# Loading a mask in 2.5 KB runs, behind the weights and both halves of the first load, with zero matmuls between the first blocks

## Chip, cores, metric

The kernel runs on one core of a Trainium2 chip. The metric is the device time of one execution in microseconds, lower being better. Executions that are called fast (not in a slow state) are compared with fast executions of the kernel before, on the same chip and in the same rounds. The profile's span is 1.6 us shorter than the time: 89.0 against 90.6 us for the kernel before.

## The reference, cut to what matters

```python
x:      (16, 512, 512) float32      weight: (512, 512) float32
scale:  0.125                       mask:   (512, 512) float32, 1 strictly below the diagonal, else 0
y = scale * matmul(x, weight)
y = where(mask == 1, y, -1e9)
return softmax(y, axis=-1)
```

The kernel relies on the mask's block shape. Of the 512 x 512 mask it reads only the four 128 x 128 blocks on the diagonal. What lies above them is a constant, and what lies below is unmasked.

## The kernel before

x is read in eight groups of 2 MB; a group is worked on in two halves of four row slots, called units here, sixteen in all. For each unit, VectorE casts to bf16, TensorE transposes (16 matmuls against the identity), VectorE and ScalarE copy the result out of PSUM (where this kernel's matmuls put it), and TensorE multiplies by W and adds the mask's "band" as one more matmul. ScalarE takes the exponential with its sum, VectorE normalises, and a DMA stores. All DMAs are issued by the SP engine, in program order.

The loads at the start:

```python
load(0, slots(0))                       # first half of group 0, 1 MB
DP = P // S                             # 16 partitions
for b in range(KT):                     # 4 mask blocks
    r = b * P
    seq(nc.sync.dma_start(diag_f32[b * DP : (b + 1) * DP],
        mask[r : r + P, r : r + P].rearrange("(p t) c -> p t c", t=S)))   # 128 pieces of 512 B
seq(nc.sync.dma_start(w_f32, weight.rearrange("(p kt) n -> p kt n", kt=KT)))   # 1 MB
load(0, slots(1))                       # second half of group 0, 1 MB
for g in range(1, X_BUFS):              # X_BUFS = 5: four more groups of 2 MB
    load(g)
```

The first units. `spin(n)` issues n matmuls of zeros, meant to raise TensorE's clock.

```python
spin(12)
...                                     # identity, band constants, spread matrices
cast(0); transpose(0); evict(0)
# diag_bf = bias made of the mask: (1 - mask) * -512, in bf16
for h in range(2):
    for j in range(2):
        pm = spread[:, h] x diag_bf[:, slots(j)]          # a matmul places the rows
        # two copies, VectorE then ScalarE, from pm into the band
w_bf = bf16(w_f32)                      # half on VectorE, half on ScalarE
cast(1)
for u in range(U + 1):                  # U = 16 units
    transpose(u + 1); cast(u + 2); evict(u + 1); multiply(u); normalise(u - 1); ...
```

TensorE runs in this order, so the multiplication of unit u + 1 stands behind the transposes of unit u + 2.

The softmax here doesn't subtract the row's maximum and nothing guards it: scores larger than these inputs give would overflow.

## Time and profile before

| | kernel before |
|---|---|
| time, median of 3 runs | 90.63 us (90.41 to 90.82) |
| span of the profile | 89.0 us |
| bytes moved by DMA | 34.95 MB, 392 GB/s over the span |
| TensorE busy | 72.1 us, 81% of the span |

In the strip of 40 slices a digit is the busy share in tenths, PEclk the clock that TensorE was granted, GB/s what the DMA engines moved. In the table by stretches, each row gives the busy time of PE, PEld, DVE, ACT and POOL with the number of instructions, and at its end the granted clock, the DMA share and the GB/s. Where a high DMA share stands beside low GB/s, the packets took longer: in the changed kernel the share is 1.06 at 133 GB/s from 11 to 12 us, with mask packets of 290 to 365 ns (medians) where the first had taken 102 ns. The prediction shows the lines.

### The profile page before, as it was taken

The page shows a single profiled execution, that of the slowest core. Times are in us where ns is not written, and L with a number is a line of the kernel's source. Part 1 is how long each engine was busy: PE and PEld are TensorE (multiplying, and loading weights), DVE is VectorE, ACT ScalarE, POOL GpSimd, SP SyncE. Part 2 cuts the span into 40 slices and gives each one's busy share as a digit, 9 for nine tenths or more (in the row PEclk, how much of TensorE's full clock was granted, in tenths as well). Part 3 has the DMA queues.
Part 4 walks back from the last instruction along what each step waited for, and adds up shares of the span by engine and source line. Part 5 has one row for each costly group of instructions (what it writes and reads, how often), then busy time and mean ns, then how long its engine had stood idle before and what let it go on. Part 6 is the DMA issues. An engine that isn't in the chain of part 4 may idle for free.

```text
span 89.0 us, 1583 instructions
## 1 busy us (share of the span) xinstructions
PE 72.1 (81%) x585; PEld 49.6 (56%) x592; DVE 61.0 (68%) x121; ACT 55.9 (63%) x154; POOL 6.6 (7%) x14
## 2 busy tenths in 40 slices
PE   4994503999999999999999999999999999980000
PEld 1324103878955659995565999556599965530000
DVE  4856785079994877999687699977689880528000
ACT  5300593445977868698687779768777977671000
POOL 7940000000200000020000002000000200000000
PEclk9999855558999999999999999999999999999555
DMA  0998999999999999999998999999999999999770
GB/s 11 390 228 328 420 464 434 405 449 420 427 434 405 434 394 427 467 427 375 456 442 383 471 427 383 464 434 397 449 427 405 449 420 420 456 401 420 324 320 15
DMA packets 3462, 34.95 MB, mean 392 GB/s; under 512 B 384, under 2 KB 896, under 8 KB 896
## 3 DMA queue, kind: packets, MB, share of 16 engines
q1 hardware_dynamic: 3456, 34.87, 94.0%
q8 instruction: 4, 0.07, 0.3%
q14 instruction: 2, 0.02, 0.0%
HBM read 18.09 MB, written 16.78 MB: 392 GB/s over the span
## 4 chain that ended last, share of the span: by engine, by line
PE 73%; DMA 10%; SPq 4%; DVE 3%; issue 1%; ACT 1%; DVEq 0%; ACTq 0%
PE py L122 48%; PE pt L98 16%; DMA xf<-in_x_dram 10%; PE py L131 8%; SPq L174 3%; DVE ot L158 1%; DVE xb L89 1%; SPq L85 1%; ACT ot L141 1%; SPq L179 1%; DVEq L290 0%; DVE rinv L156 0%; ACTq L290 0%
## 5 line engine op out<-in xcount | busy, mean ns | idle before, releaser
L122 PE MATMUL py<-w_bf,xt 128*128 128x256 bf16 (+1 forms) x249 | 51.0, 334 | 0.4
L141 ACT ACTIVATE ot<-py 128x256 f32<-128x256 f32 (+1 forms) x64 | 31.2, 493 | 8.9 <-PE py L131 8.8
L122 PEld LDWEIGHTS <-xt 128*128 128x128 bf16 x256 | 25.3, 101 | 12.8
L109 ACT COPY xt<-pt 128x1024 bf16<-128x1024 bf16 x16 | 16.2, 1012 | 12.8 <-PE pt L98 8.0
L89 DVE CAST xb<-xf 128x2048 bf16<-128x2048 f32 x16 | 19.5, 1221 | 5.8 <-DMA xf<-in_x_dram 5.8
L158 DVE TENSOR_SCALAR ot<-ot,rinv 128x256 f32<-128x256 f32 (+1 forms) x64 | 23.0, 423 | 0.7
L98 PE MATMUL pt<-ident_bf,xb 128*128 128x128 bf16 x256 | 17.8, 225 | 5.1 <-DVE xb L89 5.1
L98 PEld LDWEIGHTS <-xb 128*128 128x128 bf16 x256 | 16.6, 116 | 7.5 <-DVE xb L89 6.7
L131 PE MATMUL py<-band,ident_bf 128*128 128x256 bf16 x64 | 17.9, 280 | 0.0
L108 DVE COPY xt<-pt 128x1024 bf16<-128x1024 bf16 x16 | 11.0, 688 | 7.8 <-PE pt L98 7.8
L141 ACT ACTIVATION_READ_ACCUMULATOR ot<-py 128x1 f32 x64 | 12.8, 201 | 0.0
L131 PEld LDWEIGHTS <-ident_bf 128*128 128x128 bf16 x64 | 6.5, 101 | 4.3
L160 POOL MEMSET ot<- 4x256 f32 x4 | 1.8, 448 | 63.1 <-DVE ot L158 63.1
L190 PE MATMUL py<-zeros 128*128 128x512 bf16 x12 | 5.3, 632 | 1.2 <-DVE zeros L185 1.2
L156 DVE RECIPROCAL rinv<-rsum 128x4 f32<-128x4 f32 x16 | 2.7, 168 | 5.1 <-ACT ot L141 5.1
L198 DVE MEMSET ot<- 128x2048 f32 x2 | 3.5, 1765 | 0.8 <-issue 0.8
L190 PEld LDWEIGHTS <-zeros 128*128 128x128 bf16 x12 | 1.6, 144 | 3.9 <-issue 2.8
L233 ACT CAST band<-py 64x512 bf16<-64x512 f32 x4 | 2.3, 580 | 1.1 <-DVE band L233 1.0
L233 DVE CAST band<-py 64x512 bf16<-64x512 f32 x4 | 2.5, 675 | 0.5 <-PE py L222 0.5
L222 PE MATMUL py<-diag_bf,spread 64*128 64x512 bf16 x4 | 1.2, 412 | 0.9 <-DVE diag_bf L209 0.9
L196 POOL MEMSET band<- 64x2048 bf16 x1 | 1.8, 1800 | 0.1
L195 POOL MEMSET band<- 64x2048 bf16 x1 | 1.8, 1802 | 0.0
(14 smaller groups left out, 6.6 us busy)
## 6 DMA issues: line engine op xcount, KB each, us to landing
xf<-in_x_dram SPq DMA_DIRECT2D x7, 2048.0 KB, 17.0
out_dram<-ot SPq DMA_DIRECT2D x6, 2048.0 KB, 13.8
out_dram<-ot SPq DMA_DIRECT2D x4, 1024.0 KB, 9.6
xf<-in_x_dram SPq DMA_DIRECT2D x2, 1024.0 KB, 7.2
w_f<-in_weight_dram SPq DMA_DIRECT2D x1, 1024.0 KB, 6.9
diag_f<-in_mask_dram SPq DMA_DIRECT2D x4, 64.0 KB, 4.9
```

The source lines that it names most:

```text
L89: seq(nc.vector.tensor_copy(xb, st_x[u // 2][:, slots(u)]))
L98: nc.tensor.transpose(st_pt[u][kt // 2][:, kt % 2, t], xb[:, t].rearrange("p (k kt) -> p kt k", kt=KT)[:, kt], ident_bf,)
L108: seq(nc.vector.tensor_copy(xt[:, 0:2], pt[0]))
L109: seq(nc.scalar.copy(xt[:, 2:4], pt[1]))
L122: nc.tensor.matmul(py[:, :NC], lhsT=xt[:, kt, t], rhs=w_bf[:, kt, :NC], start=(kt == 0), stop=(kt == KT - 1),)
L131: nc.tensor.matmul(py[:, h * HB : NC], lhsT=ident_bf, rhs=band[:, h, slots(u)][:, t], start=False, stop=True, skip_group_check=True,)
L141: nc.scalar.activation(out=ot[:, t, :NC], in_=py[:, :NC], func=AF.Exp, bias=0.0, scale=float(scale), accum_out=rsum[:, t : t + 1],)
L156: seq(nc.vector.reciprocal(rinv, st_sum.pop(u)))
L158: seq(nc.vector.tensor_scalar_mul(ot[:, t, :NC], ot[:, t, :NC], rinv[:, t : t + 1]))
L190: seq(nc.tensor.matmul(idle, lhsT=zeros[:, :P], rhs=zeros, start=True, stop=True))
L198: nc.vector.memset(ots[i][:, :, HB:], 0.0)
L233: copy(band[half, h, slots(j), g * P : (g + 1) * P], pm.rearrange("p (t c) -> p t c", t=T)[half],)
```

## The change

The intent: the mask's 512 B pieces are taken to be slow packets, so two pieces that are needed and what lies between them are read as one run of 2,560 B. Row r needs 128 columns and row r + 1 the same 128 columns, 2 KB further on. This gives half as many packets but 2.5 times the bytes (655 KB instead of 262 KB). The mask no longer stands ahead of W and the second half load; both come first. The work of the second unit is brought forward, and 14 + 8 zero matmuls fill TensorE's waits.

```diff
     load(0, slots(0))
+    seq(nc.sync.dma_start(w_f32, weight.rearrange("(p kt) n -> p kt n", kt=KT)))
+    load(0, slots(1))
     DP = P // S
+    RUN = N + P
+    diag_f32 = ots[OUT_BUFS - 1].rearrange("p t n -> p (t n)")[:HP, : S // 2 * RUN]
     for b in range(KT):
-        r = b * P
         seq(nc.sync.dma_start(
                 diag_f32[b * DP : (b + 1) * DP],
-                mask[r : r + P, r : r + P].rearrange("(p t) c -> p t c", t=S),
+                bass.AP(tensor=mask.tensor, offset=mask.offset + b * P * (N + 1),
+                        ap=[[2 * N, P // 2], [1, RUN]]),
         ))
-    seq(nc.sync.dma_start(w_f32, weight.rearrange("(p kt) n -> p kt n", kt=KT)))
-    load(0, slots(1))
...
     cast(0)
     transpose(0)
+    spin(14)
     evict(0)
-    (diag_bf: one tensor_scalar of 64 x 1024)
+    (w_bf: the two casts)
+    cast(1)
+    transpose(1)
+    spin(8)
+    evict(1)
+    (diag_bf: two tensor_scalars of 64 x 512, one for each piece of a run)
     (spread matmuls and band copies, unchanged)
-    (w_bf: the two casts)
-    cast(1)
     for u in range(U + 1):              # transpose and evict of unit 1 are left out here now
```

More of the change, by code (lines that the diff above doesn't have):

```diff
@@ L67 @@
     w_bf = const.tile([P, KT, N], BF16, name="w_bf")
-    diag_f32 = const.tile([HP, S, P], FP32, name="diag_f32")
     diag_bf = const.tile([HP, S, P], BF16, name="diag_bf")
@@ L175 @@
                 diag_f32[b * DP : (b + 1) * DP],
-                mask[r : r + P, r : r + P].rearrange("(p t) c -> p t c", t=S),
-            )
-        )
-    seq(nc.sync.dma_start(w_f32, weight.rearrange("(p kt) n -> p kt n", kt=KT)))
-    load(0, slots(1))
+                bass.AP(
+                    tensor=mask.tensor,
+                    offset=mask.offset + b * P * (N + 1),
+                    ap=[[2 * N, P // 2], [1, RUN]],
+                ),
+            )
+        )
     for g in range(1, X_BUFS):
@@ L206 @@
     transpose(0)
+    spin(14)
     evict(0)
-    seq(
-        nc.vector.tensor_scalar(
-            out=diag_bf,
-            in0=diag_f32,
-            scalar1=-MASK_NEG,
-            scalar2=MASK_NEG,
-            op0=ALU.mult,
-            op1=ALU.add,
+    seq(nc.vector.tensor_copy(w_bf[:, 0:2], w_f32[:, 0:2]))
+    seq(nc.scalar.copy(w_bf[:, 2:4], w_f32[:, 2:4]))
+    cast(1)
+    transpose(1)
+    spin(8)
+    evict(1)
+    for side in range(2):
+        seq(
+            nc.vector.tensor_scalar(
+                out=diag_bf.rearrange("k (j s) c -> k j s c", s=2)[:, :, side],
+                in0=diag_f32.rearrange("k (j c) -> k j c", c=RUN)[:, :, side * N : side * N + P],
+                scalar1=-MASK_NEG,
+                scalar2=MASK_NEG,
+                op0=ALU.mult,
+                op1=ALU.add,
+            )
         )
-    )
     for h in range(2):
@@ L237 @@
                 )
-    seq(nc.vector.tensor_copy(w_bf[:, 0:2], w_f32[:, 0:2]))
-    seq(nc.scalar.copy(w_bf[:, 2:4], w_f32[:, 2:4]))
-    cast(1)
     for u in range(U + 1):
-        if u + 1 < U:
+        if 2 <= u + 1 < U:
             transpose(u + 1)
@@ L246 @@
             cast(u + 2)
-        if u + 1 < U:
+        if 2 <= u + 1 < U:
             evict(u + 1)
```

## The prediction

> **What bounds the kernel now.** I read the strip of 40 slices first, then the chain that ended last, then the table by stretches, then the DMA packets. The strip:
>
> ```profile
> PE   4994503999999999999999999999999999980000
> PEclk9999855558999999999999999999999999999555
> DMA  0998999999999999999998999999999999999770
> GB/s 11 390 228 328 420 464 434 405 449 420 427 434 405 434 394 427 467 427 375 456 442 383 471 427 383 464 434 397 449 427 405 449 420 420 456 401 420 324 320 15
> ```
>
> One slice is 2.2 us. Two rows are full from slice 9 on: PE, and DMA at about 425 GB/s. So the kernel has two bounds that lie on each other, and only a change that shortens both can shorten it much. The visible slack is in the first slices (GB/s 228, PE idle and at half clock) and in the last ones. The chain names one of the two:
>
> ```profile
> 4.73 8.77 DMA xf<-in_x_dram
> 13.49 0.02 issue
> 13.52 1.24 DVE xb L89
> 14.76 0.05 issue
> 14.80 1.90 PE pt L98 x16
> 16.70 0.85 PE py L122 x4
> ...
> 20.73 0.11 PE py L131
> 20.84 0.89 PE pt L98 x16
> ```
>
> The second half of the first load lands at 13.5 us, then the PE runs without a gap until 79.8 us. The first block of 16 transposes (I call the blocks T0, T1, ...) took 1.90 us at 14.8 and 0.89 us at 20.84, so 14.8 to 20.6 was run at half clock. After the PE come the last exponentials and normalisation (to 82.4) and the last 1 MB store, issued at 82.39 and landed 5.8 us later: 9.2 us from the PE's end to the span's end of 89.0. By stretches (engine columns, then clock, DMA share, GB/s):
>
> ```profile
> 4.00:6.00 2.00, 2.00 (x6) 0.60 (x4) 1.42 (x1) 0.00 (x0) 1.46 (x3) 1.00 1.01 308
> 6.00:8.00 2.00, 0.90 (x9) 0.41 (x8) 1.23 (x1) 0.00 (x0) 0.00 (x0) 1.00 0.88 237
> 8.00:10.00 2.00, 1.07 (x15) 0.79 (x13) 1.28 (x2) 1.01 (x1) 0.00 (x0) 1.00 1.00 418
> ...
> 12.00:14.00 2.00, 0.00 (x0) 0.00 (x0) 1.57 (x3) 1.96 (x3) 0.00 (x0) 0.50 1.01 430
> 14.00:16.00 2.00, 1.20 (x12) 1.20 (x13) 0.74 (x1) 0.17 (x1) 0.00 (x0) 0.50 0.94 401
> ```
>
> The DMA engines look busy between 5 and 8 us (share 0.9 to 1.0) but move little: that is the mask. Half-microsecond stretches from 4.5 to 8.0 add up to 844 KB where 425 GB/s would have moved 1,488 KB: 1.5 us lost. With the 0.62 us that its 262 KB need anyway, the mask occupied the DMA engines for about 2.1 us.
>
> **Why it is slow.** The idea of the change is that short packets are slow. The packet records speak against it: the first 210 or so of the 512 mask packets of 512 B took 27 ns each, against 309 ns for 8,192 B and 611 ns for 16,384 B. A line through these gives about 8 ns per packet plus 27 GB/s, so 512 B cost 27 ns instead of 19. From 5.6 to 5.9 us the same packets have medians of 52 to 60 ns, and their first slow ones stop at 75 to 76. 76 is 4 x 19. [...]
>
> ```profile
> DMA packets 204, 0.11 MB, mean 142 GB/s; under 512 B 28, under 2 KB 201, under 8 KB 201
> ```
>
> That is 5.6 to 6.4 us: mask packets almost alone, at 142 GB/s.
>
> [...] The clock here fell at 10.3 and rose at 20.6[...].
>
> **The change part by part.**
> 1. *Mask off the front of the queue.* W, landing at 11.0 us before, comes second; three 1 MB loads at 425 GB/s from about 2.3 us end near 9.8 us, so W lands around 8.5, x's second half around 11 instead of 13.5. T1 can run at 12 instead of 14.8. None of this alone moves the first multiplication, which also needs the mask's band.
> 2. *Mask in runs of 2,560 B.* 256 packets instead of 512, but 655 KB instead of 262 KB, into the same 16 partitions per DMA. [...] **about 5.2 us, 3.1 more than before**[...]. Without a port limit it would be 256 / 16 packets x 102 ns = 1.6 us, half a microsecond less than before.
> 3. *What waits behind it.* The mask lands at 9.8 + 5.2 + 1 = 16 us (a landing trails the last byte by some 1 us here: x's first half had moved by 5.0 and landed at 6.2). The second 2 MB load landed at 18.45 before (the cast that waited for it starts at 18.48); it lands at about 21.5 now.
> 4. *Zero matmuls.* 14 + 8 of 512 columns at full clock, some 0.22 us each by estimate (they were issued every 0.43 us while cold): 3.0 us after T0, 1.7 us after T1, ending near 15 us. They hold the clock until then and delay nothing, since the mask lands at 16.
> 5. *First multiplication.* From the mask: 0.7 us for the two halves of the bias conversion (one took 0.67), 0.4 for a spread matmul, about 1.3 for its two band copies (they took 0.62 and 0.58, one after the other): start at about 18.5, all four pairs 3.5 us after the spread matmuls began, as before. From 15 to 18.5 the PE does about 1 us of work[...] and the first multiplication takes up to 4.3 us, as before, to about 22.8.
> 6. *T2.* Cast from 21.5 to 22.7, T2 at 22.8 instead of 20.84. T1 is already done, but T2 and the second multiplication (3.1 us at full clock) start cold: the clock returns[...] between about 22 and 25.3. In the middle, T3 starts near 26.4 instead of 23.92: **PE path 2.5 us later**, and from there it has no slack to recover.
> 7. *The DMA bound.* 3.1 us more work in a full queue, less the 0.5 us that the queue idled at 82.5 to 83.5 waiting for the last store: **2.6 us later**.
>
> Both bounds say about 2.5 us: 90.63 + 2.5 = 93.1, plus a little where they don't line up, 93.3.
>
> **The rivals.**
> - *Packet size is the cost, not ports.* Mask 1.6 us, load two lands about 0.5 us sooner. T2 moves up to 19.3 at full clock, PE path 1.5 us earlier. But 35.3 MB in a full queue allow only 0.5 + 0.5 us: 89.7. For it: the change's design, and that half-full rates coincide with small packets. Against: the 27 ns packets.
> - *Ports limit, but the engines spread out*[...] 3.0 us, 0.9 more than before. T2 at about 20.7, the PE near its old place, DMA +0.4: about 91. For it: [...] stragglers in the packet records show that engines do drift apart.
> - *The warm clock pays off.* T1 and the first multiplication cost 3 us too much at half clock. If the PE were the only bound, that were 87.5. Against: DMA at 425 GB/s from 8 to 82 us, with a gap of just 0.5 us. I give it very little.
>
> **Range and chances.** Serial ports 0.65 (92.4 to 94.2[...]), spread-out ports 0.25 (90.5 to 92.3), packet size 0.1 (about 89.7). Weighted: 0.65 x 93.3 + 0.25 x 91.3 + 0.1 x 89.7 = 92.4; I set 92.8, nearer the main case. The limits of 2% are 88.8 and 92.4. Slower holds nearly all of the first case: 0.61; faster needs the third with more: 0.03; same 0.36.
>
> **What would show it.** Right: 110 to 150 GB/s at full DMA share for about 5 us from 10 us on; mask packets of 300 to 400 ns, not 100; the bias conversion starting at 16 and the third cast at 21 or later; a half clock somewhere between 17 and 25 us. The first step wrong: that stretch near 400 GB/s and the mask landed by 12.5. Step 6 wrong: T2 at full clock. Step 7 wrong: an end earlier than the queue's bytes allow, that is, a rate above 425 GB/s later on. The prediction fails as a whole if the mask takes under 3 us of the queue.

The sum: 5.2 us of the queue for the mask, 3.1 more than before; from this TensorE's path 2.5 us later and the queue 3.1 - 0.5 = 2.6 us later; 90.63 + 2.5 = 93.1, with a little more 93.3, and 92.8 once the rivals are weighed in. Nearly the same comes out of the packet times that the prediction gives, as an estimate: 512 packets of 76 ns on 16 engines are 2.4 us, of which 2.1 were measured (0.87); 256 packets of 4 x 94 ns (2,560 B at 27 GB/s) are 6.0 us, times 0.87 is 5.2; at 2 x 94 ns they are 3.0. The trace shows the 76 ns, about four times the 19 ns that 512 B take at 27 GB/s, but not what causes them. "Ports", here and in the expectations, is the name for a limit that goes with the number of partitions a DMA writes; no run shows what lies behind it. That the clock would be lost before 18.5 us and come back between 22 and 25.3 was the author's estimate too.

## The result, and the profile after

The changed kernel takes 94.15 us (median of 4 runs, 93.81 to 94.53) against 90.67 us for the kernel before in the same rounds. The ratio is 1.0388, with a 95% interval of 1.0338 to 1.0437: slower. A ratio here is the mean time of one kernel's fast runs over the mean of the other's fast runs in the same rounds, so it is not quite the ratio of the two medians.

The strip of the changed kernel (a slice is 2.3 us):

```profile
PE   4949738299999999999999999999999999990000
PEclk9999999955599999999999999999999999999655
DMA  0999999999999999999999999999999999999790
GB/s 28 382 407 428 242 140 170 403 425 432 418 410 446 439 410 403 428 460 421 393 428 439 432 425 403 439 439 432 432 410 418 446 439 418 418 446 393 336 375 21
```

The front of the queue is better than before: 382, 407 and 428 GB/s in slices 1 to 3, where the kernel before had 390, 228 and 328. Then three slices fall to 242, 140 and 170 at full DMA share. DMA is full again from slice 7 on, PE from slice 8. By single microseconds of the same kernel:

```profile
9.00:10.00 1.00, 1.00 (x6) 0.41 (x5) 0.00 (x0) 1.00 (x2) 0.00 (x0) 1.00 0.92 386
10.00:11.00 1.00, 1.00 (x5) 0.29 (x3) 0.00 (x0) 0.00 (x1) 0.00 (x0) 1.00 1.15 200
11.00:12.00 1.00, 0.03 (x1) 0.00 (x0) 0.15 (x1) 0.00 (x0) 0.00 (x0) 1.00 1.06 133
12.00:13.00 1.00, 0.00 (x0) 0.00 (x0) 1.00 (x1) 0.00 (x0) 0.00 (x0) 1.00 1.08 133
13.00:14.00 1.00, 0.86 (x15) 0.87 (x16) 0.27 (x2) 0.00 (x0) 0.00 (x0) 1.00 1.54 191
14.00:15.00 1.00, 1.00 (x9) 0.53 (x8) 0.50 (x1) 0.74 (x1) 0.00 (x0) 1.00 1.35 175
15.00:16.00 1.00, 0.94 (x5) 0.31 (x4) 0.00 (x0) 0.27 (x1) 0.00 (x0) 1.00 0.57 117
16.00:17.00 1.00, 0.00 (x0) 0.00 (x0) 0.00 (x0) 0.00 (x0) 0.00 (x0) 1.00 0.81 311
```

Between 10 and 16 us the queue moves 117 to 200 GB/s. The first of the mask's packets of 2,560 B (9.9 to 10.2 us) took 102 ns, but the mean of all 256 is 290 ns. In the steady part their medians are 290 to 380 ns.

The chain of waits of the changed kernel (start, duration, what) shows what this did to TensorE:

```profile
4.82 12.24 DMA ot<-in_mask_dram
17.18 0.77 DVE diag_bf L223 x2
18.40 0.69 DVE band L247
19.12 0.59 ACT band L247
19.75 1.01 PE py L121 x4
...
24.18 1.38 PE pt L97 x16
...
27.74 0.89 PE pt L97 x16
...
83.61 0.60 ACT ot L140
```

The same view of the kernel before, at the places that are compared:

```profile
23.92 0.89 PE pt L98 x16
...
79.79 0.60 ACT ot L141
```

The chain goes through the mask, not through x: it lands at 17.1, its bias and band take until 19.7, and only then does the first multiplication begin, at half clock (granted 0.50 from 18.2 to 25.1 us). In the kernel before, the block of transposes T2 started at 20.84 and T3 at 23.92. Here T2 starts at 24.18 and T3 at 27.74: 3.8 us later. From there the two kernels run alike, and the last exponential starts at 83.61 instead of 79.79, again 3.8 us later. The span grew by 3.6 us.

### The profile page after: what moved, and what is told of

The parts are those of the page before. It is cut to its first block, busy times and chain, and to the rows that moved or that the text cites. A ratio compares the mean times of both kernels' runs of the same rounds, so it can differ in the third digit from the quotient of the medians.

```text
span 92.6 us, 1636 instructions
## 1 busy us (share of the span) xinstructions
PE 76.8 (83%) x614; PEld 51.2 (55%) x614; DVE 61.3 (66%) x122; ACT 55.8 (60%) x154; POOL 6.6 (7%) x14
## 3 DMA queue, kind: packets, MB, share of 16 engines
HBM read 18.48 MB, written 16.78 MB: 381 GB/s over the span
## 4 chain that ended last, share of the span: by engine, by line
PE 69%; DMA 13%; SPq 4%; DVE 3%; ACT 1%; issue 1%; DVEq 0%; ACTq 0%
PE py L121 47%; PE pt L97 14%; DMA ot<-in_mask_dram 13%; PE py L130 8%; SPq L178 2%; DVE ot L157 1%; SPq L84 1%; DVE diag_bf L223 1%; DVE band L247 1%; ACT ot L140 1%; ACT band L247 1%; SPq L168 1%; DVEq L301 0%; PE py L236 0%; DVE rinv L155 0%
## 5 line engine op out<-in xcount | busy, mean ns | idle before, releaser
L196 PE MATMUL py<-zeros 128*128 128x512 bf16 x34 | 9.5, 438 | 1.2 <-DVE zeros L191 1.2
L196 PEld LDWEIGHTS <-zeros 128*128 128x128 bf16 x34 | 3.5, 110 | 5.8 <-issue 2.2
L236 PE MATMUL py<-diag_bf,spread 64*128 64x512 bf16 x4 | 1.7, 554 | 2.0 <-DVE diag_bf L223 2.0
L223 DVE TENSOR_SCALAR diag_bf<-ot 64x512 bf16<-64x512 f32 x2 | 0.8, 416 | 2.7 <-DMA ot<-in_mask_dram 2.7
## 6 DMA issues: line engine op xcount, KB each, us to landing
xf<-in_x_dram SPq DMA_DIRECT2D x7, 2048.0 KB, 20.3
ot<-in_mask_dram SPq DMA_DIRECT2D x4, 160.0 KB, 11.2
```

The costliest lines, as they stand in the source:

```text
L196: seq(nc.tensor.matmul(idle, lhsT=zeros[:, :P], rhs=zeros, start=True, stop=True))
```

## The experiments

Two theories are told apart first.

- **Partitions** (the "port theory"). A mask DMA that writes few partitions is held to a rate that goes with their number. A longer run to the same 16 partitions then costs in proportion to its bytes.
- **Packets.** Short packets are slow, whatever they are written to. Then longer runs should have helped, and the loss must come from the new order.

A third claim of the prediction is tested along the way: that the kernel lies on two bounds at once, so that TensorE's gains are taken back by the DMA queue.

To compare the mask's cost I use one measure for all runs. I take the bytes moved in a stretch of 9 us around the mask (8 to 17 us, or 4 to 13 us where the mask comes early), subtract the mask's own, divide the rest by 425 GB/s, and call what is left of the 9 us the mask's **occupancy** of the queue. A run without any mask gives -0.3 us by this measure, so it is good to about 0.3 us. "T3" is the start of the fourth block of transposes (that of unit 3) in the chain of waits, "last exp" the start of the last exponential there.

| run | mask DMAs | occupancy, us | T3 | last exp | span | median, us | ratio to before |
|---|---|---|---|---|---|---|---|
| before | 4 x 16 partitions, 512 B | 2.0 | 23.92 | 79.79 | 89.0 | 90.67 | 1 |
| changed | 4 x 16, 2,560 B | 5.6 | 27.74 | 83.61 | 92.6 | 94.15 | 1.0388 |
| runs_first | 4 x 16, 2,560 B, old place | 5.6 | 26.73 | 82.60 | 92.8 | 94.84 | 1.0427 |
| short_pieces | 4 x 16, 512 B, new place | 1.9 | 22.62 | 78.49 | 89.0 | 90.78 | 0.9999 |
| wide_runs | 4 x 32, 2,560 B | 2.7 | 23.46 | 79.33 | 89.8 | 91.93 | 1.0127 |
| ports_runs | 2 x 128, 2,560 B | 2.4 | 23.20 | 79.07 | 90.0 | 91.70 | 1.0076 |
| wide_short | 4 x 32, 512 B | 1.7 | 22.29 | 78.16 | 88.5 | 90.42 | 0.9963 |
| ports_short | 4 x 128, 512 B | 2.0 | 22.74 | 78.61 | 89.4 | 91.19 | 0.9991 |
| one_dma (wrong result) | 1 x 128, 512 B | 0.6 | 22.24 | 78.11 | 89.2 | 91.0, one run | - |
| no_mask2 (wrong result) | none | -0.3 | 22.20 | 78.07 | 88.8 | 90.48 | 0.9939 |
| no_zeros | as changed | 5.1 | 26.51 | 82.38 | 92.8 | 94.71 | 1.0391 |
| short_no_zeros | as short_pieces | 1.8 | 24.93 | 80.80 | 89.5 | 91.38 | 1.0022 |

The runs were made in three lots, in which the kernel before had medians of 90.67, 91.08 and 90.98 us, so runs of different lots are compared by their ratios; their spans and medians must not be subtracted from each other. One run of the kernel before (92.29 us) was slow and is left out of the ratios.

### The runs alone, at the old place: runs_first

```diff
 (the kernel before)
-    mask in 512 B pieces, behind the first half load
+    mask in 2,560 B runs, behind the first half load
-    diag_bf in one tensor_scalar
+    diag_bf in two
```

> The kernel before with one thing changed: the mask in runs of 2,560 B over 16 partitions, at its old place behind the first half load; no zeros, old order. Theory: the runs are the whole loss, so the mask takes 5 us instead of 2 there too, W lands near 14 us, x's second half near 16.5, and the time is 93.0 to 94.3. If the new place behind W and both halves were the loss, this stays at 90.6 to 91.2.

Measured: 94.84 us, ratio 1.0427 (1.0370 to 1.0483). The occupancy is 5.6 us, as in the changed kernel. One row of the strip, here of GB/s, shows the trough where the mask now is:

```profile
GB/s 39 364 202 145 190 413 477 410 410 452 438 417 403 424 452 389 434 434 424 431 431 438 410 410 424 424 424 438 431 431 431 424 424 424 438 438 392 424 215 21
```

That is 0.5 us above the range expected. The run length alone makes the whole loss: the two intervals overlap, so that it makes more than the whole is not shown. The new order and the zeros are not to blame.

### The short pieces at the new place: short_pieces

```diff
 (the changed kernel)
-                bass.AP(tensor=mask.tensor, offset=..., ap=[[2 * N, P // 2], [1, RUN]]),
+                mask[r : r + P, r : r + P].rearrange("(p t) c -> p t c", t=S),
-    diag_bf in two tensor_scalars
+    diag_bf in one
```

> The changed kernel, with only the mask's pieces put back to 512 B (262 KB in 512 packets, still 16 partitions per DMA, still behind W and both halves). Port theory: the bytes [...]at about 130 GB/s set the cost, so the mask takes about 2.1 us of the queue instead of 5.0, the second 2 MB load lands near 18.5 us instead of 21.7, and the time is 90.0 to 91.0. Packet theory: twice as many packets at an equal or higher cost, so no faster than the changed kernel's 94.15.

Measured: 90.78 us, ratio 0.9999 (0.9956 to 1.0042), as the theory of partitions said. Undoing the runs undoes the loss. It also shows that the rest of the change brings nothing that counts, although it does what it was meant to do: TensorE holds full clock from 5.9 us to the end of its work, and T3 starts 1.3 us before that of the kernel before.

### The same runs to twice the partitions: wide_runs

The mask rows go four to a partition instead of eight, so that each DMA writes 32 partitions. The packets are the same 256 of 2,560 B, read from the same addresses. The spread matmuls get a 128-row matrix for each of the four (h, j).

```diff
 (the changed kernel)
-    DP = P // S                              # 16
+    DP = P // T                              # 32
-    diag_bf = const.tile([HP, S, P], BF16);  spread = const.tile([HP, 2, P], BF16)
+    diag_bf = const.tile([P, T, P], BF16);   spread = const.tile([P, 2, 2, P], BF16)
-            lhsT=spread[:, h],    rhs=diag_bf[:, slots(j)]
+            lhsT=spread[:, h, j], rhs=diag_bf
```

> The changed kernel with the same 256 packets of 2,560 B, but each mask DMA spread over 32 partitions instead of 16 (mask rows four to a partition, the spread matmul over 128 partitions). Port theory: [...]packets of about 190 ns instead of 330, the mask about 3.0 us of the queue[...], time 91.3 to 92.3. Rival, that the read from HBM or the number of bytes sets the rate: 133 GB/s and about 5 us as in the changed kernel, time within 0.5 us of 94.15.

Measured: 91.93 us, ratio 1.0127. The packets' mean fell from 290 to 168 ns, and in the steady part their medians are 166 to 198 ns, against twice 94 ns (2,560 B at 27 GB/s, the line through the packet times of the kernel before). The occupancy halved, from 5.6 to 2.7 us. The rows by microseconds:

```profile
10.00:11.00 1.00, 1.00 (x6) 0.29 (x3) 0.00 (x0) 0.08 (x1) 0.00 (x0) 1.00 0.98 277
11.00:12.00 1.00, 0.11 (x1) 0.00 (x0) 0.80 (x1) 0.00 (x0) 0.00 (x0) 1.00 1.08 236
```

236 GB/s stands where the changed kernel had 133. Bytes, packets and source addresses are equal, only the number of partitions that a DMA writes has doubled: this is what decides. The rival (HBM reads or bytes alone) is out. In the steady part the packet times are about four times 94 ns or less with 16 partitions (290 to 380 ns) and about two times with 32 (166 to 198 ns). Why the number of partitions counts, no run shows.

### The same runs to all partitions: ports_runs

```diff
 (wide_runs)
-    for b in range(KT):
+    for j in range(T // 2):
-            diag_f32[b * DP : (b + 1) * DP]
+            diag_f32[:, j * RUN : (j + 1) * RUN]
-            offset=mask.offset + b * P * (N + 1),  ap=[[2 * N, P // 2], [1, RUN]]
+            offset=mask.offset + j * 2 * N,        ap=[[T * N, P // T], [P * (N + 1), KT], [1, RUN]]
```

> The changed kernel with the same 256 runs of 2,560 B (655 KB), but in two DMAs that each write all 128 partitions. If ports limit the runs (330 ns a packet on 16 partitions, 190 ns on 32), the packets fall to about 102 ns and the mask takes 1.6 to 1.9 us of the queue; time 89.8 to 90.6. If the strided read from HBM limits beyond that, it stays near the 3 us of wide_runs and the time near 91.9.

Measured: 91.70 us, ratio 1.0076, occupancy 2.4 us: between the two. From 11.8 us on, its packets took 102 ns, as hoped. But from 10.4 to 11.8 they had medians of 126 to 251 ns and were few, with a DMA share of 0.7: the engines were partly idle. What held them up in that first part is not settled. It was the first of the two DMAs: counting the increments of its semaphore, it landed 2.1 us after the load before it, the second 0.8 us after the first, which is 410 GB/s. The step from 32 to 128 partitions brings much less than that from 16 to 32.

### The same for the short pieces: wide_short, ports_short, one_dma

wide_short is wide_runs with 512 B pieces. ports_short has four DMAs, each with one row per partition over all 128 partitions. one_dma reads 512 pieces in a single DMA, always the first 128 columns. Its output is wrong, which doesn't matter for the time.

```diff
 (wide_short)
-    four DMAs, each: diag_f32[b * 32 : (b + 1) * 32] <- mask[b * 128 : ..., b * 128 : ...]
+    ports_short: four DMAs, each: diag_f32[:, j] <- row j of every partition's four
+    one_dma:     one DMA: diag_f32 <- mask.rearrange("(p t) c -> p t c", t=T)[:, :, :P]
```

> As wide_runs, but with 512 B pieces: 262 KB over 32 partitions per DMA. Port theory: about 1.2 us of the queue, the second 2 MB load landing near 17.5 us, time 89.0 to 89.9, faster than the kernel before. Packet theory: as slow as short_pieces.

> 512 B pieces in four DMAs that each write all 128 partitions. short_pieces (16 partitions) and wide_short (32) both needed about 2.0 us for the mask, so ports seem not to limit short pieces. If a rate of packets or a fixed cost per DMA limits them: again 2.0 us, time 90.2 to 90.7. If ports did: about 0.9 us, time 89.3 to 89.9.

> The 512 pieces of 512 B in a single DMA over 128 partitions, always columns 0 to 127 (wrong result on purpose). A fixed cost of about 0.5 us per DMA would leave some 0.9 to 1.1 us for the mask; a limit per packet of about 60 ns an engine leaves 2.0 us.

Measured: wide_short 90.42 us (0.9963, interval 0.9912 to 1.0015), ports_short 91.19 us (0.9991). The expectation for wide_short was missed. Its packets did get shorter, 31 ns on average against 49 in short_pieces, but the occupancy stayed at 1.7 us: now the engines had gaps, with a DMA share of 0.53 and 0.43 from 10 to 12 us. In one_dma, at 1.0 us from first packets to nearly the last, the packets averaged 27 ns and the occupancy was 0.6 us, less than either case expected. So 512 B packets are not slow in themselves, and the number of partitions is not all that held the kernel before. Four small DMAs in a row cost some 2 us here whether they write 16, 32 or 128 partitions, and a single one less than half of that. one_dma differs in two ways, though: one DMA instead of four, and the same columns for all rows. What the four lose between their packets stays open. It is not an equal price for each DMA: in ports_short the first mask DMA landed 1.8 us after the load before it, and the other three 0.2 us apart. Two half microseconds of that run, the first with the engines mostly idle:

```profile
10.50:11.00 0.50, 0.50 (x4) 0.10 (x1) 0.16 (x1) 0.00 (x0) 0.00 (x0) 1.00 0.19 26
12.00:12.50 0.50, 0.38 (x7) 0.38 (x8) 0.06 (x1) 0.00 (x0) 0.00 (x0) 1.00 1.82 650
```

In wide_short the four landed 0.3 to 0.7 us apart, the loss spread over all of them.

### No mask at all: no_mask, no_mask2

```diff
 (the changed kernel)
-    the four mask DMAs
+    no_mask:  nc.gpsimd.memset(diag_f32, 1.0), conversions kept
+    no_mask2: nc.vector.memset(diag_bf, 0.0) in place of the conversions
```

> The changed kernel without the mask's DMAs, the tile filled by a memset (wrong result on purpose). It shows what the rest of the change is worth and the floor of the DMA bound. Theory of two bounds: the PE starts its second block of transposes near 17.5 us, 3.3 us earlier than in the kernel before, but 34.7 MB in a full queue end only 2.1 + 0.5 us earlier: about 88.0. Rival, that the PE alone is the bound: 87.3 or less.

no_mask took 91.23 us (1.0051) and is a failed experiment: the memset that replaced the DMA did harm of its own. Its four runs fall into two pairs (90.80 and 90.81, 91.66 and 91.86 us), and the profile is of the slowest, so what follows is shown for that execution only.

```profile
5.73 2.22 POOL L199 MEMSET ot<- 64x2560 f32 x1
5.93 3.11 DVE L88 CAST xb<-xf 128x2048 bf16<-128x2048 f32 x1 [0.51 <-DMA xf<-in_x_dram]
```

The cast beside the GpSimd memset took 3.11 us instead of 1.23. TensorE then waited, lost its clock at 8.1 us, and the 14 zeros that stood in front of the next transposes took 5.25 us, all but the last microsecond at half clock, instead of 3.19 in the changed kernel. Zeros in a fixed number are a hazard of their own: once the clock was lost here, they came 0.43 us apart instead of 0.22 and delayed the work behind them.

> Again no mask DMA (wrong result on purpose), now with a short DVE memset of the bias tile, because no_mask's GpSimd memset held a DVE cast up to 3.1 us and spoiled it. Two bounds: the PE starts its third block near 20.5 us instead of 23.9, but 34.7 MB in a full queue end only 2.1 + 0.5 us earlier, 87.8 to 88.5. PE as the only bound: 87.2 or less.

no_mask2 took 90.48 us, ratio 0.9939 (0.9903 to 0.9975). **This is the run that my model of the end did not foresee.** TensorE's path became 1.7 us shorter (last exponential at 78.07), yet the time by the ratio only some 0.6 us. That a second bound takes the gain back is right, but the queue should have ended 2.6 us earlier and did not. The trace shows two losses. One is a trough at 28 to 31 us that the kernel before doesn't have:

```profile
27.00:28.00 1.00, 1.00 (x18) 0.88 (x16) 0.53 (x1) 0.73 (x3) 0.00 (x0) 1.00 1.60 492
28.00:29.00 1.00, 1.00 (x7) 0.52 (x6) 0.96 (x4) 1.00 (x2) 0.00 (x0) 1.00 1.07 213
29.00:30.00 1.00, 1.00 (x7) 0.49 (x5) 1.00 (x4) 0.72 (x3) 0.00 (x0) 1.00 0.48 115
30.00:31.00 1.00, 1.00 (x6) 0.49 (x5) 1.00 (x1) 0.71 (x3) 0.00 (x0) 1.00 0.88 303
```

The 16 KB packets there took up to 1.6 us instead of 0.61, and against 425 GB/s these 4 us lose about 1.4 us (an estimate from the rows). In one_dma the same happens at 29 to 31 us; it is not explained. The other is at the end: the final completion packets of the last store came one by one from 84.5 to 87.4 us, so they lay some 3 us apart, and the last sets the end. In the kernel before 11 of 16 came from 86.1 to 86.4 and the last at 87.9.

### The zeros: no_zeros, short_no_zeros

```diff
 (the changed kernel; short_pieces)
-    spin(14)
-    spin(8)
```

> The changed kernel without the 22 zero matmuls in between. Theory: they end before the mask lands and the clock is lost anyway, so their removal changes little: 93.7 to 94.7, with the first block of the second transposes at half clock. If they are worth their place, it is slower by a microsecond or more.

> short_pieces, which kept full clock throughout, without the 22 zero matmuls. Here they can matter: without them the clock falls near 10 us and the PE's third block of transposes starts 2 to 3 us later than in short_pieces (22.5), near 25. Since the DMA queue hides up to about 1.3 us of that, 91.0 to 92.5 against 90.78.

Measured: no_zeros 94.71 us, ratio 1.0391, which cannot be told from the changed kernel's 1.0388. In the changed kernel the zeros end near 16 us, the mask lands at 17.1, and the clock falls at 18.2 in spite of them. Without the zeros T3 even came 1.2 us earlier (the mask landed 0.4 us earlier, and the clock returned at 22.7 instead of 25.1), and the time did not follow. short_no_zeros took 91.38 us, ratio 1.0022, against 0.9999 with zeros: the intervals (0.9984 to 1.0060 and 0.9956 to 1.0042) overlap. Here the zeros do their work, since without them T3 starts 2.3 us later. The time hardly answers. The chains of the two runs, short_pieces first:

```profile
19.53 0.91 PE pt L98 x16
22.62 0.89 PE pt L98 x16
```

```profile
21.67 1.07 PE pt L98 x16
24.93 0.89 PE pt L98 x16
```

TensorE was 2.3 us later to the end (last exponential at 80.80 instead of 78.49), and the time by the ratios some 0.2 us longer, which is within the noise. This is the second bound, shown from the other side. When TensorE is early, the last store waits in a full queue: in short_pieces the span ends 10.5 us after the last exponential starts, in the changed kernel 9.0 us.

### The mask issued by ACT: act_short

```diff
 (short_pieces)
-            nc.sync.dma_start(diag_f32[...], mask[...])
+            nc.scalar.dma_start(diag_f32[...], mask[...])
```

> short_pieces with the four mask DMAs issued by ACT at the start, so that they share the engines with the loads instead of holding a place in their queue. If the mask's short packets are taken in turn with the large ones, the mask lands between 6 and 12 us and costs the queue about 1 us instead of 2: 89.6 to 90.4. If a stalled packet stalls the engine whatever its ring: 90.5 to 91.

Measured: 96.09 us, ratio 1.0547 (1.0482 to 1.0612), the slowest of all and outside both ranges expected. The idea was right in that the mask's packets were taken in turn with the large ones, and wrong in what this means. From 6 to 12 us, 237 mask packets and 224 of 8 KB started: equal numbers, as if one of each were taken in turn. When the loads' packets become 16 KB long, the turn takes longer still (147 mask packets and 154 of 16 KB from 12 to 19 us). The last mask packet ended at 18.9 us:

```profile
20.31 0.69 DVE L218 TENSOR_SCALAR diag_bf<-diag_f 64x1024 bf16<-64x1024 f32 x1 [4.97 <-DMA diag_f<-in_mask_dram]
```

The bias began at 20.3 us, 3.1 us later than in the changed kernel, and T3 at 30.87. It also moved only 356 GB/s from 36 to 60 us, which the mask cannot explain, and which stays open.

### What stays open

Why four small DMAs in a row cost about 2 us even to 128 partitions, and why there the first of them takes most of it. Why the queue stumbles at 28 to 31 us in no_mask2 and one_dma. Why the last completions lie up to 3 us apart at the end. No correct version tried is clearly faster than the kernel before. The best is wide_short, and its interval of 0.9912 to 1.0015 includes 1.

## Why the prediction was right

The forecast was slower, 92.8 us with a range of 90.4 to 94.2; measured 94.15, close to the upper limit. The sign held, and so did the cause: the mask's long runs into 16 partitions. The size was short by 1.35 us of the forecast and by 0.85 us of the main case's 93.3; that it still fell inside the range, by 0.05 us, is partly luck. By its own steps:

1. *Mask off the front.* Mostly right. W was cast at 8.2. The second half of x was late: its last packets ended between 9.9 and 10.5 us, but the cast that waited for it started at 11.85, not near 11, so T1 ran at 13.1 instead of 12. It landed at 11.8 here, at 11.2 in short_pieces and at 10.8 in ports_short, so with the slow runs even a load ahead of the mask landed later.
2. *The mask's cost.* That the runs into few partitions cost it is shown by wide_runs and runs_first. The size was 5.6 us instead of 5.2 (3.6 more than before instead of 3.1). The overlap measured on the short pieces (2.1 us of the 2.4 that 76 ns a packet make, 0.87) was smaller for the runs (5.6 of the 6.0 that 4 x 94 ns make).
3. *What waits behind it.* It landed at 17.1, not 16: its last packet ended at 15.6 instead of 15.0, and the landing trailed that by 1.5 us instead of 1. The second 2 MB load let its cast start at 21.77 (21.5 expected).
4. *Zeros.* Right that they delay nothing and don't keep the clock until it is needed (no_zeros: no difference). They ended at 16, not 15, because T1 was later.
5. *First multiplication.* At 19.75 instead of 18.5, following the mask's landing, and at half clock, as foreseen.
6. *T2 and T3.* T2 at 24.18 (22.8 expected) and T3 at 27.74 (26.4 expected). The clock came back at 25.1, inside the 22 to 25.3 that I gave (an estimate). **PE path 3.8 us later instead of 2.5.** This is the mis-sized term: the first multiplication started 1.2 us late, and T2 stands behind it on TensorE, so T2 came from it and not from the x load.
7. *The DMA bound.* About 2.6 us were predicted. The data's end moved from 87.9 to 91.4 us, 3.5 us. No_zeros shows that this bound lies close to the other: its TensorE path was 1.2 us shorter than the changed kernel's, its time no shorter (ratio 1.0391). In the changed kernel the queue did run low before the last store (311 GB/s from 86 to 87 us), so TensorE's path set the end there.

Some of the working was wrong, without harm to the result. I took the clock to follow how busy TensorE had been in the microseconds before, and the profiles give no threshold for this. In the kernel before TensorE was 53% busy from 6.93 to 10.34 us, with a granted clock of 1.00, and the clock stood at 0.50 from there to 20.58; from 13.76 to 17.17 it was 69% busy and the clock stayed at 0.50. In the changed kernel it was 50% busy from 11.42 to 14.83 and the clock stayed at 1.00 until 18.24; from 18.24 to 21.66 it was 97% busy and the clock stayed at 0.50, until 25.07. I read the slow half of the mask in the kernel before as the effect of few partitions alone. wide_short and ports_short show that with more partitions it still takes 1.7 to 2.0 us, so something else costs too. And the rival sums that give a time for a shorter mask (89.7 if packet size is the cost) were too low: by no_mask2, even no mask at all gains only 0.6%. My account of a full queue left out the trough and the late last completions that this run shows.

## What to carry to other kernels

Before you lengthen the runs of a small load to save packets, compare what a packet costs at its fastest (here 27 ns for 512 B, 102 ns for 2,560 B) with what it costs in place, and count the partitions that each DMA writes: here a packet of 2,560 B took 290 ns on average into 16 partitions per DMA and 168 ns into 32. A small load can delay what is queued behind it (here the cast of the second 2 MB load started at 21.77 instead of 18.48 us), and its own waiters as well, so look at what the first multiplication waits for last: moving other loads ahead of it gained nothing here while it still gated the work (W landed at 8.2 instead of 11.0 us, and the first multiplication started at 19.75 instead of 16.70). Where two bounds lie on each other, a gain on one must be checked against the end of the other: TensorE was up to 1.7 us earlier in these runs for at most 0.6% of the time (no_mask2).
